# Row sums of a 64 MiB tensor: partition 4a+b holds block a+32b in place of block 4a+b

## The chip, the cores and the metric

The kernel runs on one core of one Trainium2 chip. The metric is the device time of one execution in microseconds, the median of several runs. Before the change it is 160.3 us (three runs, 160.28 to 160.54).

A core has 128 partitions of on-chip memory, five engines with queues of their own (here DVE, ACT, POOL and SP have work; PE has none) and sixteen DMA engines, which move data between HBM and the partitions. SP issues every DMA copy of this kernel.

## The reference

```python
def setup_inputs():
    batch, seq, dim = 32, 512, 1024
    return {
        "x": np.random.randn(batch, seq, dim).astype(np.float32),
        "divisor": float(dim),
    }

def reference(x: np.ndarray, divisor: float) -> np.ndarray:
    return (np.sum(x, axis=-1) / divisor).astype(np.float32)
```

The input is 16,384 rows of 1,024 float32 numbers, 67.1 MB. The output is the sum of each row, divided by 1,024: 16,384 numbers, 64 KiB.

## The kernel before, in words

**How rows are dealt out.** Each of the 128 partitions adds up 128 rows. The rows lie in HBM in two parts. The first part is 128 blocks of F = 15 rows; partition p holds block p (`x_first`, `o_first`). The second part is 128 blocks of W = 113 rows; partition p holds block p here too. Of the 113 rows, the first M = 97 are the main rows (`x_main`, `o_main`) and the last L = 16 the closing rows (`x_last`, `o_last`). Each of these names is an access pattern of the HBM tensor, written out by hand: an offset, and pairs of step and count in elements, the slowest first. `x_main`, for instance, goes in 128 steps of 113 rows and takes contiguous numbers at each.

**Loads.** The list `loads` holds ten copies in the order of issue: two rows per partition, five times 16 rows and once 15 rows of the main part; then the 15 rows of the first part; then the first 10.6 rows and the next 3.7 rows of the closing part. They go in turn into three buffers of 64 KiB per partition (`bulk`). Two more copies bring the rest of the closing part into `pa` (1.3 rows, 5,376 B per partition) and `pb` (0.4 of a row, 1,664 B). Within a partition the bytes of a copy are contiguous in HBM and on chip.

**What sets the order.** It is written out by hand, with a semaphore for each buffer. The first two copies are issued at L116; the function `start_loads_at_once` moves them to the very start of SP's program, ahead of the barrier with which the engines begin. The other eight of the list are issued at L144: the third waits for the first one's data, and each later one waits until DVE (and ACT, where it had a share) is done with the buffer it goes to, and until the earlier data of that buffer have landed. `pa` (L145) and `pb` (L146) are issued right behind. Then SP waits for POOL and issues the store of the 15-row part's results (L148), waits until the copy to `pa` has landed and ACT has added up the head of row 14, issues the store of the main results (`res`, L150), waits for the last two sums, and issues the store of the closing results (`fin`, L238). At the very end it waits for all stores.

**Who adds up.** DVE reduces each list entry's rows with one instruction (L215), but for four rows of the 15-row main load and six of the first part's, which ACT adds up with one activation per row (L183). The closing rows are shared between ACT and DVE; DVE takes them row by row, adding the two halves of a row (`both_halves`, L205), and its last instruction adds up `pb` with what came before of the last row. POOL multiplies `res` and `res0` by 1/1024 (L157, L161); closing rows are scaled as they are added up.

Of the kernel before, what the change touches and what calls it, by code (L numbers as in the profile page):

```python
# [35 lines left out]
def kernel(  # L36
# [6 lines left out]
    nc = tc.nc  # L43
    nc.at_finalize(start_loads_at_once)
    xf = x.flatten_outer_dims()
    N, D = xf.shape
    P = nc.NUM_PARTITIONS
# [4 lines left out]
    F, L = 15, 16  # L52
    M = J - F - L
    W = M + L
    x_first = bass.AP(tensor=x.tensor, offset=0, ap=[[F * D, P], [1, F * D]])
    x_main = bass.AP(tensor=x.tensor, offset=P * F * D, ap=[[W * D, P], [1, M * D]])
    x_last = bass.AP(tensor=x.tensor, offset=P * F * D + M * D, ap=[[W * D, P], [1, L * D]])
    o_first = bass.AP(tensor=out.tensor, offset=0, ap=[[F, P], [1, F]])
    o_main = bass.AP(tensor=out.tensor, offset=P * F, ap=[[W, P], [1, M]])
    o_last = bass.AP(tensor=out.tensor, offset=P * F + M, ap=[[W, P], [1, L]])  # L60

    def room(name, *shape):
        return nc.alloc_sbuf_tensor(name, [P, *shape], F32).ap()
# [10 lines left out]
    c10, c14, c15 = 640, 288, 608  # L74
    ends = [0, 10 * D + c10, 14 * D + c14, 15 * D + c15, 16 * D]
    tail = room("tail", 7 * 256)
    pa, row14 = tail[:, 256 : 256 + ends[3] - ends[2]], tail[:, 255 : 256 + D - c14]
    pb = room("pb", 512)[:, : D - c15 + 2]
# [8 lines left out]
    loads = []  # L87
    sems = {}

    def sem(name):  # L90
        sems[name] = nc.alloc_semaphore(name)
        return sems[name]

    in_bulk = [sem(f"in_bulk{i}") for i in range(3)]
    in_pa, in_pb = (sem(f"in_{n}") for n in ("pa", "pb"))
# [8 lines left out]
    for rows_of, src, dst in ((main, x_main, res), (first, x_first, res0)):  # L104
        j = 0
        for rows, on_act in rows_of:
            t = bulk[len(loads) % 3][:, : rows * D]
            loads.append((t, in_bulk[len(loads) % 3], src[:, j * D : (j + rows) * D], on_act, dst[:, j : j + rows]))
            j += rows
    for k in range(2):  # L110
        t = bulk[len(loads) % 3][:, : ends[k + 1] - ends[k]]
        loads.append((t, in_bulk[len(loads) % 3], x_last[:, ends[k] : ends[k + 1]], 0, None))


    for t, s, src, *_ in loads[:2]:
# [18 lines left out]
    for k, (t, s, src, *_) in enumerate(loads):  # L134
# [7 lines left out]
                nc.sync.wait_ge(act, done_act[k - 3])  # L142
            nc.sync.wait_ge(s, arrived[k] - 16)
        nc.sync.dma_start(out=t, in_=src).then_inc(s, 16)  # L144
    nc.sync.dma_start(out=pa, in_=x_last[:, ends[2] : ends[3]]).then_inc(in_pa, 16)  # L145
    nc.sync.dma_start(out=pb[:, : D - c15], in_=x_last[:, ends[3] : ends[4]]).then_inc(in_pb, 16)  # L146
    nc.sync.wait_ge(pool, 3)
    nc.sync.dma_start(out=o_first, in_=res0).then_inc(out_first, 16)  # L148
    nc.sync.wait_ge(in_pa, 17)
# [4 lines left out]
    k = len(main) - 1  # L154
# [31 lines left out]
    for k, (t, s, src, on_act, dst) in enumerate(loads[:-2]):  # L186
        rows = t.shape[1] // D
# [23 lines left out]
    for k, (t, s, src, on_act, dst) in enumerate(loads[:-2]):  # L211
        m = t.shape[1] // D - on_act
        nc.vector.wait_ge(s, arrived[k])
        rows = t[:, : m * D].rearrange("p (r d) -> p r d", d=D)
# [65 lines left out]
```

## Time and profile before

| what | value |
|---|---|
| median of the runs | 160.3 us |
| span of the profiled execution, first to last instruction | 159.3 us |
| DVE busy | 116.7 us, 73% of the span |
| ACT busy | 18.6 us, 12% |
| POOL busy | 1.0 us |
| read from HBM | 67.11 MB |
| share of the sixteen DMA engines' time with a packet | 98.1% |

The profile is of one execution, whose time outside the profiler is not known; the span is the time from its first to its last instruction, 1.0 us under the median of the runs. The chain of work that ended last is followed back from the last instruction, at each step to what released it; a line of it that says DMA means that an engine waited for that copy to land. In the lists by time, SPq stands for SP's queue, on which copies are issued; the time of such a line is that of the issue, not of the transfer. The windows give the share of time in which the DMA engines had a packet on its way, and the bytes that they moved. A landing is the moment when one of the sixteen DMA engines reports its part of a copy; a copy has landed with the sixteenth.

### The profile page before, as it was taken

Reading aid. Unit: us, or ns where it says so; the run is one execution under the profiler, and the core shown is the slowest. Engines: PE = TensorE matmul, PEld = TensorE weight load, DVE = VectorE, ACT = ScalarE, POOL = GpSimd, SP = SyncE. Lnnn points to the kernel's source line nnn. Section 1 sums busy time; section 2 is a strip of 40 time slices with the busy share of each in tenths; the row PEclk is TensorE's granted clock in tenths of the full one; section 3 lists DMA queues with packets and bytes.
Section 4 is the critical chain, followed back from the end, with each engine's and each line's share of the span. In section 5 each row is a group of like instructions: output and inputs, shape, how many; then the busy total and the mean of one; then the engine's idle time right before and its main releaser. Section 6 shows DMA issues by size and latency. Waiting matters only on the chain.

```text
span 159.3 us, 144 instructions
## 1 busy us (share of the span) xinstructions
DVE 116.7 (73%) x32; ACT 18.6 (12%) x35; POOL 1.0 (1%) x7
## 2 busy tenths in 40 slices
DVE  0500009999499994999949999499989990399296
ACT  3000000000000000000000000000009100392196
POOL 0000000000000000000000000000000001000000
DMA  8996996996996997979969969969996999889894
GB/s 296 494 527 263 527 527 263 527 527 263 527 527 263 527 444 346 527 313 477 527 263 527 527 263 527 494 278 463 494 494 262 478 494 494 350 350 525 344 401 154
DMA packets 2160, 67.18 MB, mean 422 GB/s; under 512 B 624, under 2 KB 752, under 8 KB 880
## 3 DMA queue, kind: packets, MB, share of 16 engines
q1 hardware_dynamic: 2160, 67.18, 98.1%
HBM read 67.11 MB, written 0.07 MB: 422 GB/s over the span
## 4 chain that ended last, share of the span: by engine, by line
DMA 67%; DVE 30%; another core or an unknown queue 1%; issue 0%
DMA bulk<-in_x_dram 67%; DVE res L215 29%; DVE bulk L205 1%; DVE tail L205 0%; DVE pb L205 0%; DVE fin L205 0%
## 5 line engine op out<-in xcount | busy, mean ns | idle before, releaser
L215 DVE TENSOR_REDUCE res<-bulk 128x16 f32<-128x16384 f32 (+3 forms) x8 | 110.0, 13754 | 37.7 <-DMA bulk<-in_x_dram 37.7
L183 ACT ACTIVATE junk<-bulk 128x1024 f32<-128x1024 f32 (+1 forms) x16 | 15.6, 973 | 137.2 <-DMA bulk<-in_x_dram 137.2
L205 DVE CUSTOM_DVE_ANT_0 bulk<-bulk 128x512 f32<-128x512 f32 (+1 forms) x9 | 5.5, 665 | 3.1 <-DMA bulk<-in_x_dram 3.1
L183 ACT ACTIVATION_READ_ACCUMULATOR junk<-bulk 128x1 f32 x16 | 3.0, 187 | 0.0
L183 ACT ACT_TABLE_LOAD x1 | 1.3, 1283 | 1.9 <-PEq L119 1.9
L157 POOL TENSOR_SCALAR res<-res 128x97 f32<-128x97 f32 x1 | 0.5, 465 | 129.8 <-DVE res L215 129.8
L205 DVE DVE_READ_ACCUMULATOR2_ANT fin<- 128x1 f32 x10 | 0.8, 82 | 0.0
L183 ACT ACTIVATE junk<-tail 128x737 f32<-128x737 f32 x1 | 0.8, 789 | 0.0
L205 DVE CUSTOM_DVE_ANT_0 bulk<-bulk,part 128x192 f32<-128x192 f32 x1 | 0.4, 420 | 0.3 <-DMA bulk<-in_x_dram 0.3
L205 DVE CUSTOM_DVE_ANT_0 tail<-tail 128x304 f32<-128x304 f32 x1 | 0.5, 476 | 0.0
L205 DVE CUSTOM_DVE_ANT_0 pb<-pb 128x209 f32<-128x209 f32 x1 | 0.4, 379 | 0.1
L161 POOL TENSOR_SCALAR res<-res 128x15 f32<-128x15 f32 x1 | 0.3, 262 | 15.6 <-DVE res L215 15.6
L183 ACT ACTIVATION_READ_ACCUMULATOR junk<-tail 128x1 f32 x1 | 0.2, 187 | 0.0
L153 POOL MEMSET pb<- 128x2 f32 x1 | 0.1, 99 | 1.5 <-POOLq L119 1.5
L261 POOL MEMSET const-bfloat16-1.0<- 128x1 bf16 x1 | 0.1, 101 | 0.0
L261 POOL MEMSET const-uint8-127<- 128x1 uint8 x1 | 0.1, 101 | 0.0
L261 POOL MEMSET const-float32-0.0<- 128x1 f32 x1 | 0.1, 98 | 0.2 <-issue 0.2
L261 POOL MEMSET const-float32-1.0<- 128x1 f32 x1 | 0.1, 98 | 0.0
L205 DVE DVE_READ_ACCUMULATOR2_ANT pb<- 128x1 f32 x1 | 0.1, 84 | 0.0
L205 DVE DVE_READ_ACCUMULATOR2_ANT part<- 128x1 f32 x1 | 0.1, 83 | 0.0
## 6 DMA issues: line engine op xcount, KB each, us to landing
bulk<-in_x_dram SPq DMA_DIRECT2D x2, 7680.0 KB, 39.3
bulk<-in_x_dram SPq DMA_DIRECT2D x1, 5440.0 KB, 32.0
bulk<-in_x_dram SPq DMA_DIRECT2D x1, 1872.0 KB, 23.5
bulk<-in_x_dram SPq DMA_DIRECT2D x1, 1024.0 KB, 4.6
tail<-in_x_dram SPq DMA_DIRECT2D x1, 672.0 KB, 24.7
pb<-in_x_dram SPq DMA_DIRECT2D x1, 208.0 KB, 24.8
bulk<-in_x_dram SPq DMA_DIRECT2D x5, 40.8
out_dram<-res SPq DMA_DIRECT2D x1, 48.5 KB, 1.6
```

The lines of the kernel that those rows point to most:

```text
L153: nc.gpsimd.memset(pb[:, D - c15 :], 0.0).then_inc(pool)
L157: nc.gpsimd.tensor_scalar_mul(out=res, in0=res, scalar1=scale).then_inc(pool)
L161: nc.gpsimd.tensor_scalar_mul(out=res0, in0=res0, scalar1=scale).then_inc(pool)
L183: nc.scalar.activation(scratch, src, COPY, scale=by, accum_out=dst).then_inc(count)
L205: return nc.vector.tensor_tensor_reduce(out=src[:, :h], in0=src[:, :h], in1=src[:, h:], scale=by, scalar=ahead, op0=ADD, op1=ADD, accum_ou ...
L215: nc.vector.reduce_sum(out=dst[:, :m], in_=rows, axis=AX).then_inc(dve)
L261: nc = _bacc.Bacc("TRN2", target_bir_lowering=False, num_devices=1)
```

## The change

In the 113-row part the partitions hold other blocks. Where partition p held block p, partition 4a + b (a from 0 to 31, b from 0 to 3) now holds block a + 32b. So partitions 0, 1, 2, 3 hold blocks 0, 32, 64, 96, and partitions 4 to 7 hold blocks 1, 33, 65, 97. The access patterns in HBM say this with one pair more: 32 steps of one block, and in each four steps of 32 blocks. The stores of `res` and `fin` use the same mapping, so that each sum goes to its row. On the chip's side nothing is addressed otherwise, and the 15-row part is as before. Slices of the patterns take the last axis whatever the number of axes.

```diff
     x_first = bass.AP(tensor=x.tensor, offset=0, ap=[[F * D, P], [1, F * D]])
-    x_main = bass.AP(tensor=x.tensor, offset=P * F * D, ap=[[W * D, P], [1, M * D]])
-    x_last = bass.AP(tensor=x.tensor, offset=P * F * D + M * D, ap=[[W * D, P], [1, L * D]])
+    G = P // 4
+    x_main = bass.AP(tensor=x.tensor, offset=P * F * D, ap=[[W * D, G], [G * W * D, 4], [1, M * D]])
+    x_last = bass.AP(tensor=x.tensor, offset=P * F * D + M * D, ap=[[W * D, G], [G * W * D, 4], [1, L * D]])
     o_first = bass.AP(tensor=out.tensor, offset=0, ap=[[F, P], [1, F]])
-    o_main = bass.AP(tensor=out.tensor, offset=P * F, ap=[[W, P], [1, M]])
-    o_last = bass.AP(tensor=out.tensor, offset=P * F + M, ap=[[W, P], [1, L]])
+    o_main = bass.AP(tensor=out.tensor, offset=P * F, ap=[[W, G], [G * W, 4], [1, M]])
+    o_last = bass.AP(tensor=out.tensor, offset=P * F + M, ap=[[W, G], [G * W, 4], [1, L]])
...
-            loads.append((t, in_bulk[len(loads) % 3], src[:, j * D : (j + rows) * D], on_act, dst[:, j : j + rows]))
+            loads.append((t, in_bulk[len(loads) % 3], src[..., j * D : (j + rows) * D], on_act, dst[:, j : j + rows]))
...
-        loads.append((t, in_bulk[len(loads) % 3], x_last[:, ends[k] : ends[k + 1]], 0, None))
+        loads.append((t, in_bulk[len(loads) % 3], x_last[..., ends[k] : ends[k + 1]], 0, None))
...
-    nc.sync.dma_start(out=pa, in_=x_last[:, ends[2] : ends[3]]).then_inc(in_pa, 16)
-    nc.sync.dma_start(out=pb[:, : D - c15], in_=x_last[:, ends[3] : ends[4]]).then_inc(in_pb, 16)
+    nc.sync.dma_start(out=pa, in_=x_last[..., ends[2] : ends[3]]).then_inc(in_pa, 16)
+    nc.sync.dma_start(out=pb[:, : D - c15], in_=x_last[..., ends[3] : ends[4]]).then_inc(in_pb, 16)
```

## The prediction

> **What bounds the kernel now.** I read the profile's page first, for who is busy. The vector engine is busy for 73% of the span, the DMA engines for all of it.
>
> ```profile
> span 159.3 us, 144 instructions
> DVE 116.7 (73%) x32; ACT 18.6 (12%) x35; POOL 1.0 (1%) x7
> DMA packets 2160, 67.18 MB, mean 422 GB/s; under 512 B 624, under 2 KB 752, under 8 KB 880
> q1 hardware_dynamic: 2160, 67.18, 98.1%
> ```
>
> 98.1% is the share of sixteen engines' time in which a packet was on its way. Next I read the windows by stage, which say where the rest is lost (columns: stretch, its length, busy time of DVE, ACT and POOL, granted clock, DMA share, GB/s).
>
> ```profile
> 1.00:4.60 3.60, 0.00 (x0) 1.28 (x1) 0.10 (x1) 1.00 1.48 580
> 4.60:43.28 38.68, 19.51 (x2) 0.00 (x0) 0.00 (x0) 1.00 1.00 434
> 43.28:81.98 38.70, 34.44 (x3) 0.00 (x0) 0.00 (x0) 1.00 1.00 434
> 81.98:119.83 37.85, 34.44 (x2) 0.00 (x0) 0.00 (x0) 1.00 0.99 428
> 119.83:138.00 18.17, 11.90 (x2) 4.28 (x9) 0.47 (x1) 1.00 0.96 417
> ```
>
> A packet's bytes are booked where it starts, so the first window is too high (580) and those at the end too low; the long windows are right. From 4.6 to 82 us the sixteen engines move 434 GB/s, share 1.00. The trace's list of packets gives the same: a packet of 65,536 B (one partition's share of a sixteen-row load; 640 of them) takes 2.418 us at the least and at the median, 27.1 GB/s an engine and 434 GB/s for sixteen. So 67.11 MB need 154.7 us, and nothing but the bytes, the start and the end decide the time. The chain of work and the instructions in order of time (both: start, length, what) give these two ends.
>
> ```profile
> 0.00 4.58 DMA bulk<-in_x_dram
> ...
> 131.75 23.51 DMA bulk<-in_x_dram
> ...
> 157.41 0.02 issue
> 157.44 0.38 DVE pb L205
> ```
>
> ```profile
> 0.00 0.85 SPq L116 DMA_DIRECT2D bulk<-in_x_dram  x2
> ...
> 157.85 0.33 SPq L238 DMA_DIRECT2D out_dram<-fin  x1
> ```
>
> At the start SP issues the first load in 0.376 us (the shorter of the two at L116; the second takes 0.424), and the list of packets has the first one at 1.00 us: 0.62 us later. At the end the last input bytes land at 157.41, DVE adds them up by 157.82, SP issues the store of `fin` from 157.85 to 158.18, its packets run from 158.68 to 158.88, and it lands at 159.26. The span of this execution is 159.3; the median of the runs is 160.3, so 1.0 us lies outside the span, and I carry that over.
>
> Between these ends, 157.41 - 1.00 - 154.7 = 1.7 us are lost. The list of packets accounts for half: summed over packets, each against the shortest of its size, an engine spends 0.48 us too much in the first load's 8,192 B packets (309 ns undisturbed, 602 on average for the first sixteen), 0.18 in those of 61,440 B, 0.15 in those of 65,536 B. The rest is gaps and engines that do not end together (the last load's sixteen landings are spread over 0.56 us).
>
> **The change, part by part.** No instruction of DVE, ACT, POOL or PE is added, removed or moved, and SP issues the same fifteen copies in the same order with the same bytes. Three things differ.
>
> *Which bytes a partition gets.* Nothing in the sums depends on it: every row is added up within a partition, and results are written by the same mapping. Cost 0 on the compute engines: 8 reductions (110.0 us), 16 activations (15.6) as before, all under the loads but for the last 0.4 us, which depend on no address.
>
> *Where in HBM the engines read at one time.* A step from one partition to the next was one block of 113 rows, 452 KiB; now it is 32 blocks, 14.1 MiB, and a step of four partitions, which was 1,808 KiB, is 452 KiB. Every run is as long as before (16 rows, 64 KiB). Bounds: a gain of at most the 1.7 us lost now; a loss of as much as the stretch seen now, 0.8 us, doubled (nearest rows: the 8,192 B packets, which are hardest hit). The row nearest to most of these bytes is the 65,536 B packet, which with the old addresses is at its floor in the median and 3.6 ns above it in the mean: there is next to nothing to win in the bulk. I take -0.05 us (a tenth of the first load's stretch).
> The Trainium skill bears on this in "DMA: Bandwidth & Descriptors", section "Latency and other measured facts": copies whose partitions lie a large power of two apart lose up to half their rate, and a pad of 4 KiB brings it back. Neither 452 nor 1,808 KiB is such a pitch, so by that rule the sum has 0 here in place of -0.05; the trace of before agrees for 1,808 KiB with its 434 GB/s.
>
> *The form of the copies.* In the new program the DRAM side of thirteen of the fifteen copies (the eleven input loads of the 113-row part and the stores of `res` and `fin`) has three steps, 32 x 4 x length, where it had two, 128 x length; the load and the store of the 15-row part keep theirs. The program built from before also marks each copy as one whose pattern is worked out ahead; the thirteen lose that mark. SP's sequencer then has more to work out per issue. No row shows an issue of that kind. Bounds from the rows: at the least 0; at the most one whole further issue, that is 0.376 us for the first load and 0.332 for the last store. A gain is excluded, since no part of an issue goes away. A copy that is issued right behind another is the nearest row for an issue that finds its work not ready: 0.43 and 0.44 us at L145 and L146 against 0.328 for one that stood alone, so 0.1 us is a lower mark; a whole address pattern more on each side is nearer to a second issue than to that, so I take 0.25 us each, and keep 0 and the full issue for the range.
>
> Now copy by copy. The first load (L116): nothing is ahead of it, so its 0.25 us shift the first packet from 1.00 to 1.25 and with it every byte, since the engines never rest: **+0.25**. The second load at L116, queued behind it, is issued by about 1.35 in place of 0.85; the first load keeps the engines to 4.3, so 3 us cover it. SP's barrier stands behind both: the other engines would start at 2.4 rather than 1.9, and DVE has nothing to do before 4.6. The eight at L144: each is issued 18 us or more ahead of its first byte (at 4.6 and 6.9 for bytes from 23.6 and 42.9; at 131.7 for 150.3); this lead covers 0.25 us many times over. What waits behind them on SP are the next copies, which wait for DVE anyway: 95.6 us in seven waits. L145 and L146 are issued at 132.1 and 132.6 and land at 157: covered by some 23 us. The store of the 15-row part is unchanged. The store of `res` (L150) is issued at 156.89 for 0.34 us, and SP waits from 157.23 to 157.85 for `fin`: 0.62 us of cover, so 0.25 more are free, and at twice the cost still; were that gone, the store of `fin` would slip. Its landing, at 158.45, would be 158.70, before that of `fin`. The store of `fin` (L238) is the last thing on the path and has no cover: **+0.25**. Its 64 B runs and the 388 B runs of `res` go to the same outputs from other partitions; their packets take 11 and 24 ns, and I put 0 on that.
>
> Sum: 159.3 + 0.25 + 0.25 - 0.05 = 159.75 span, plus 1.0 outside it: **160.8 us**, 0.3% above 160.3.
>
> **The rivals.** *The addresses win more than the issue costs (faster).* The stretch of the first load falls away where neighbouring DMA engines read 452 KiB apart in place of 1,808, and engines finish closer together. For it: the 0.48 us of the first packets and the 0.56 us spread at the end are there to be won. Against: the first packets of any engine are also the ones that start from an idle memory, which no address cures, and the long packets are at their floor. At half of the 1.7 us, 0.85, and 0.5 for the issues: 160.3 - 0.35 = 159.95. It decides when the saving passes 0.5 us; without any issue cost it would be 159.45.
>
> *The form is free and the addresses do not matter (no change).* For it: SP's issue may be overlapped with the 0.62 us to the first packet; before's packets show no sign of addresses. Then 160.3. Against: SP's 0.33 to 0.44 us are visible and serial at both ends.
>
> *The copies are dealt out unevenly.* Sixteen landings per copy say that sixteen engines share 128 partitions. If 32 x 4 were dealt out so that two engines serve what one port takes, or eight engines did all the work, the thirteen copies' 113/128 of 154.7 us would double: 136.6 more, 297 us. It decides already when one engine gets a ninth partition: an eighth of 136.6 is 17 us, 177 us. For it: no row shows such a copy. Against: 32 and 128 are both whole multiples of sixteen.
> The Trainium skill's "DMA: Bandwidth & Descriptors", section "Why a DMA increments its semaphore by 16 and not by 1", states that the number of engines is the largest up to 16 that divides the slowest steps of both sides; by it 32 and 128 give 16, and the time stays 160.8. Its section "The descriptor swizzle" gives engine 0 partitions 0 to 3 and 32 to 35, which 32 steps of four can be cut into; no run here shows it yet.
>
> **How the numbers follow.** Forecast 0.60; faster by addresses 0.22; no change 0.10; uneven 0.08 (with anything else that slows the stream by a per cent or more). A measurement of this kernel tells 0.2% (0.3 us) from no change. The forecast's own range is 160.3 to 161.1 (0 to 0.71 for the two issues, with the stretch a little either way); of it about a tenth falls within 0.2%. The low end goes to the faster rival's 159.95, rounded to 159.9, which leaves out the half of it that saves more. The high end: both issues doubled, 161.0, and the stretch of 0.8 us grown by three quarters, 161.6. What is left out: about 0.11 below and 0.08 above. Faster 0.22; same 0.16 (0.10 and a tenth of the forecast); slower 0.62 (0.54 and 0.08).
>
> **What would show it.** SP's issue of the first load should take about 0.6 us in place of 0.376, that of `fin` likewise, and the other loads' issues too, but not the one of the 15-row load. The first landing at 4.58 should come at about 4.8, the last reduction start about 0.2 us later, and the windows from 5 to 82 us should still say 434 GB/s. If the issues stand at 0.33 us, the step on the form is wrong; if the long windows move off 434, the step on the addresses is wrong; if the first landing comes before 4.58 with longer issues, the first packets have won by the addresses.

## The result, and the profile after

The changed kernel takes 161.45 us (median of five runs, 161.31 to 161.57) against 160.33 us for the kernel before on the same chip: a ratio of 1.0067, 95% interval 1.0055 to 1.0079. It is slower by about 1.1 us, on the side that was forecast, inside the stated range (159.9 to 161.6), but above the forecast of 160.8 and above the forecast's own range (160.3 to 161.1).

The page of the changed kernel shows the same work and the same busy times:

```profile
span 160.0 us, 144 instructions
DVE 116.7 (73%) x32; ACT 18.7 (12%) x35; POOL 1.0 (1%) x7
q1 hardware_dynamic: 2160, 67.18, 97.6%
```

The packets and bytes are those of before; only their share of the span fell, from 98.1% to 97.6%. The windows by stage (stretch, its length, busy time of DVE, ACT and POOL, granted clock, DMA share, GB/s) say that the long middle is as fast as it was:

```profile
4.60:43.28 38.68, 19.51 (x2) 0.00 (x0) 0.00 (x0) 1.00 1.00 432
43.28:81.98 38.70, 34.44 (x2) 0.00 (x0) 0.00 (x0) 1.00 1.00 434
81.98:119.83 37.85, 34.44 (x2) 0.00 (x0) 0.00 (x0) 1.00 1.01 436
```

In the trace's list of packets a 65,536 B packet still takes 2.418 us at the median, and each copy still reports sixteen landings. So the time came from the two ends. First the chain of work, then SP's queue by time (start, length, what):

```profile
0.00 5.21 DMA bulk<-in_x_dram
...
131.97 23.54 DMA bulk<-in_x_dram
...
157.70 0.02 issue
157.72 0.38 DVE pb L206
```

```profile
0.00 1.30 SPq L117 DMA_DIRECT2D bulk<-in_x_dram  x2
...
132.56 0.60 SPq L146 DMA_DIRECT2D tail<-in_x_dram  x1
133.20 0.60 SPq L147 DMA_DIRECT2D pb<-in_x_dram  x1
148.49 0.35 SPq L149 DMA_DIRECT2D out_dram<-res  x1
157.14 0.61 SPq L151 DMA_DIRECT2D out_dram<-res  x1
158.14 0.57 SPq L239 DMA_DIRECT2D out_dram<-fin  x1
```

The two first issues take 1.30 us together, where they took 0.85, and the first load lands at 5.21 in place of 4.58. L149, the store of the 15-row part, keeps its old form and its old 0.35 us; L146, L147, L151 and L239, all in the new form, take 0.57 to 0.61. For the eight loads that are issued later, the answer by line gives least, median and greatest duration in ns, first the kernel before and then the changed one:

```profile
L144 SPq DMA_DIRECT2D bulk<-in_x_dram x8: 328/328/328, 4.6 to 131.7; - x8
```

```profile
L145 SPq DMA_DIRECT2D bulk<-in_x_dram x8: 372/535/541, 5.2 to 132.0; - x8
```

The one at 372 ns is the 15-row load, which kept two steps and its mark; the other seven went from 328 to about 535.

### The profile page after: what moved, and what is told of

Its sections match the earlier page's. It is cut to its first block, busy times and chain, and to the rows that moved or that the text cites. A ratio compares the mean times of both kernels' runs of the same rounds, so it can differ in the third digit from the quotient of the medians.

```text
span 160.0 us, 144 instructions
## 1 busy us (share of the span) xinstructions
DVE 116.7 (73%) x32; ACT 18.7 (12%) x35; POOL 1.0 (1%) x7
## 3 DMA queue, kind: packets, MB, share of 16 engines
q1 hardware_dynamic: 2160, 67.18, 97.6%
## 4 chain that ended last, share of the span: by engine, by line
DMA 67%; DVE 30%; another core or an unknown queue 1%; issue 0%
DMA bulk<-in_x_dram 67%; DVE res L216 29%; DVE bulk L206 1%; DVE pb L206 0%; DVE tail L206 0%; DVE fin L206 0%
```

## The experiments

All are small edits of the kernel before or of the changed one. In each the ratio is to runs of the kernel before on the same chip. It is not the quotient of the two medians given beside it; microseconds given as "about" are worked out from the ratio, and the difference of the medians is up to 0.14 us away from them. The theory held going in is "issue": all the time is lost at the two ends, because an unmarked copy in three steps reaches its first packet later. The main rivals are "bulk addresses" (the new blocks cost or win time in the long loads) and, within "issue", whether the mark, the third step or the new blocks are what costs.

### The first load alone

```diff
+    G = P // 4
+    x_new = bass.AP(tensor=x.tensor, offset=P * F * D, ap=[[W * D, G], [G * W * D, 4], [1, W * D]])
...
-            loads.append((t, in_bulk[len(loads) % 3], src[:, j * D : (j + rows) * D], on_act, dst[:, j : j + rows]))
+            loads.append((t, in_bulk[len(loads) % 3], x_new[..., : rows * D] if not loads else src[:, j * D : (j + rows) * D], on_act, dst[:, j : j + rows]))
```

> The kernel before, with the first load alone (two rows) in the new three-step form and from the new blocks; the sums of these two rows therefore stand in other rows' places. Theory 'issue' (the time is lost at the two ends, in SP's issue of an unmarked three-step copy): issue of the first load about 0.67 us, first landing at about 5.2 us, all later landings of the bulk 0.3 to 0.6 late, 160.8 to 160.9 us. Theory 'bulk addresses' (the time is lost in the long loads): 160.3 us, first landing at 4.6. Theory 'free start' (only the end costs): 160.3.

Measured: 161.06 us against 160.42, ratio 1.0031 (1.0021 to 1.0041), about 0.50 us. The chain and SP's queue:

```profile
0.00 5.58 DMA bulk<-in_x_dram
...
157.90 0.02 issue
```

```profile
0.00 1.26 SPq L118 DMA_DIRECT2D bulk<-in_x_dram  x2
...
158.34 0.33 SPq L240 DMA_DIRECT2D out_dram<-fin  x1
```

The first issue takes 0.633 us and the first packet is at 1.41 us. The long loads are the old ones, and still everything down to the last load ends late. The first landing was expected at about 5.2 us and came at 5.58: that is 4.17 us after the first packet, where the kernel before has 3.58 and 3.82 in its two profiles (the second one follows below). The issue theory accounts for the first packet's 0.41 us and not for the rest of this landing's delay. One copy of 1 MB out of 67 does this: "bulk addresses" and "free start" fall as explanations of this half.

### The last store alone

```diff
-    o_last = bass.AP(tensor=out.tensor, offset=P * F + M, ap=[[W, P], [1, L]])
+    G = P // 4
+    o_last = bass.AP(tensor=out.tensor, offset=P * F + M, ap=[[W, G], [G * W, 4], [1, L]])
```

> The kernel before, with the last store (fin) alone in the new form; its sums therefore stand in other rows' places. Theory 'issue': the issue takes 0.57 in place of 0.33 us, the landing comes 1.8 in place of 1.4 us after its start, 160.5 to 160.7 us. Theory 'bulk addresses': 160.3.

Measured: 160.92 us against 160.42, ratio 1.0027 (1.0016 to 1.0038), about 0.43 us; the number expected was too low, the mechanism is as expected. SP's queue:

```profile
0.00 0.85 SPq L117 DMA_DIRECT2D bulk<-in_x_dram  x2
...
157.68 0.63 SPq L239 DMA_DIRECT2D out_dram<-fin  x1
```

The issue is 0.30 us longer (0.632 for 0.332), and the landing comes 1.86 us after its start instead of 1.41, so 0.45 later. Nothing lies behind this store, so all of it is paid.

### The ten loads between, without the ends

`x_new` is that of the first experiment.

```diff
-            loads.append((t, in_bulk[len(loads) % 3], src[:, j * D : (j + rows) * D], on_act, dst[:, j : j + rows]))
+            loads.append((t, in_bulk[len(loads) % 3], x_new[..., j * D : (j + rows) * D] if loads and src is x_main else src[:, j * D : (j + rows) * D], on_act, dst[:, j : j + rows]))
...
-        loads.append((t, in_bulk[len(loads) % 3], x_last[:, ends[k] : ends[k + 1]], 0, None))
+        loads.append((t, in_bulk[len(loads) % 3], x_new[..., M * D + ends[k] : M * D + ends[k + 1]], 0, None))
...
-    nc.sync.dma_start(out=pa, in_=x_last[:, ends[2] : ends[3]]).then_inc(in_pa, 16)
-    nc.sync.dma_start(out=pb[:, : D - c15], in_=x_last[:, ends[3] : ends[4]]).then_inc(in_pb, 16)
+    nc.sync.dma_start(out=pa, in_=x_new[..., M * D + ends[2] : M * D + ends[3]]).then_inc(in_pa, 16)
+    nc.sync.dma_start(out=pb[:, : D - c15], in_=x_new[..., M * D + ends[3] : M * D + ends[4]]).then_inc(in_pb, 16)
```

> The kernel before, with the new form and the new blocks in ten input loads of the 113-row part, and not in the first load nor in the stores; the sums of these ten loads' rows therefore stand in other rows' places. Theory 'issue': 160.3 us, for SP's issues of the ten loads (0.53 to 0.60 us in place of 0.33 to 0.44) are covered. Theory 'bulk addresses', as a loss: 161 or more. As a gain (the 0.3 us that the changed kernel won back between 44 and 120 us come from the addresses): 159.9 to 160.1, with the landing at about 119.8 earlier by 0.3.

Measured: 160.50 us against 160.42, ratio 1.0005 (0.9996 to 1.0015): no difference. This holds both the longer issues of ten loads and the new blocks for 98% of the 113-row part's bytes. The issues did get longer, and they are covered:

```profile
4.84 127.19 SPq L146 DMA_DIRECT2D bulk<-in_x_dram  x8
132.09 0.60 SPq L147 DMA_DIRECT2D tail<-in_x_dram  x1
132.74 0.60 SPq L148 DMA_DIRECT2D pb<-in_x_dram  x1
```

```profile
4.60:43.28 38.68, 19.50 (x2) 0.00 (x0) 0.00 (x0) 1.00 1.00 434
43.28:81.98 38.70, 34.44 (x2) 0.00 (x0) 0.00 (x0) 1.00 1.00 434
```

So longer issues and new addresses together are worth at most 0.04% on the faster side and 0.15% on the slower, and no run here points to a version faster than the kernel before. The three parts, 0.31, 0.27 and 0.05%, each with an interval of about 0.1% either way, add up to 0.63%, against 0.67% for the whole change. The store of `res`, also in the new form there, is in none of the three; in the changed kernel its issue ends at 157.75 us, before that of `fin` begins at 158.14, and it lands at 159.13, before `fin` at 159.94.

### Old form and old blocks, without the mark

```diff
     nc = tc.nc
+    nc.dge_precook = False
```

> The kernel before in everything, two steps and old blocks, but with the mark of a pattern worked out ahead taken from all fifteen copies. Theory 'issue, by the mark': SP's issues take 0.55 to 0.67 us, first landing at about 5.2, landing of fin 1.7 to 1.8 us after its issue, 161.0 to 161.5 us. Theory 'issue, by the three steps': issues stay at 0.33 to 0.44 and the time at 160.3. Theory 'addresses' (first packets slower because of the new blocks): longer issues shift the first packet by 0.3, first landing 4.9, 160.6 to 160.9.

Measured: 161.16 us against 160.42, ratio 1.0039 (1.0027 to 1.0051), about 0.63 us, without a single address or step changed. SP's queue:

```profile
0.00 1.21 SPq L117 DMA_DIRECT2D bulk<-in_x_dram  x2
...
148.38 0.51 SPq L149 DMA_DIRECT2D out_dram<-res  x1
157.06 0.50 SPq L151 DMA_DIRECT2D out_dram<-res  x1
158.05 0.47 SPq L239 DMA_DIRECT2D out_dram<-fin  x1
```

"By the mark" holds for most of the cost: issues that stood at 328 ns take 472, and the first packet of the first load comes at 1.35 us. The lengths were expected at 0.55 to 0.67 and are 0.47 to 0.60, since the third step is missing here; it adds its own part (535 ns in the changed kernel where this one has 472). The first load lands at 5.19, as the mark's theory expected, and not at 4.9. No run here has three steps with the mark.

### The kernel before, profiled again

> The kernel before, unchanged, profiled once more, to see how far its first profile stands for it. If the 0.18 us of stretched 61,440 B packets and the late sixteenth landing (0.31 us behind the fifteenth at 101.5 and 119.8 us) were of that one execution: a span of about 159.0 us, run time 1.35 us above the span as in e1 to e4, no such gap between the last two landings. If they belong to the old blocks: the span stays at 159.3 and the gap shows again. Time 160.3 to 160.4 either way.

Measured: 160.49 us against 160.53, ratio 0.999 (0.998 to 1.000), which also shows how far two samples of one kernel can differ. Its span is 159.1 us, 1.34 us below that run's time of 160.42; in the changed kernel and in the first four experiments the same difference is 1.33 to 1.35 us.

```profile
0.00 4.83 DMA bulk<-in_x_dram
...
131.52 23.51 DMA bulk<-in_x_dram
...
157.20 0.02 issue
157.22 0.38 DVE pb L205
```

The sixteenth landing at 119.6 us is 0.04 us behind the fifteenth, not 0.31, and the stretch of the 61,440 B packets is 0.03 us an engine, not 0.18. The first, second and fourth experiment, which read the long loads from the old blocks, do not show it either (0.03 to 0.11 us and 0.03 to 0.04 us). So these two marks were of the first profile's one execution. What looked like 0.4 us won back by the changed kernel between 44 and 120 us (0.60 us late at 43.86, 0.22 at 120.03) was the reference losing it: against the repeated profile the changed kernel is 0.38 us late at 43.86 and 0.45 at 120.03.

### The changed kernel with its start undone

The 15-row part becomes a 17-row part, and the first load takes its two rows from there, in the old form. All results are at their places.

```diff
-    F, L = 15, 16
+    F, L = 17, 16
...
-    main = [(2, 0)] + [(16, 0)] * 5 + [(15, 4)]
-    first = [(15, 6)]
+    main = [(16, 0)] * 5 + [(15, 4)]
+    first = [(2, 0), (15, 6)]
...
-    for rows_of, src, dst in ((main, x_main, res), (first, x_first, res0)):
-        j = 0
+    for rows_of, src, dst, j in (
+        (first[:1], x_first, res0, 0), (main, x_main, res, 0), (first[1:], x_first, res0, first[0][0])
+    ):
...
-    k = len(main) - 1
+    k = len(main)
...
-    k += len(first)
+    k += 1
```

> The changed kernel with one part undone: the 15-row part becomes a 17-row part (the other 111 rows), and the first load takes its two rows from it, in two steps and with the mark; all other loads of the 111-row part and the stores of res and fin keep the new form. Theory 'issue': the cost of the start goes and that of the last store stays: first issue 0.38 us, first landing 4.6 to 4.8, fin landing 1.8 us after its issue, 160.7 to 160.9 us. Theory 'it is the new blocks or their pitch': 161.3 to 161.5 as the changed kernel.

Measured: 160.95 us against 160.53, ratio 1.0020 (1.0010 to 1.0030), where the changed kernel stands at 1.0067. The time is a little above the 160.7 to 160.9 expected, on a chip where the kernel before stands at 160.53. The first issue is back at 0.382 us and the first packet at 1.03; the store is as slow as in the changed kernel:

```profile
0.00 5.00 DMA bulk<-in_x_dram
```

```profile
0.00 1.07 SPq L118 DMA_DIRECT2D bulk<-in_x_dram  x2
...
157.77 0.57 SPq L240 DMA_DIRECT2D out_dram<-fin  x1
```

The first landing, at 5.00, is later than the 4.6 to 4.8 expected; the issue theory does not say why, and I leave it open (the 8,192 B packets were stretched by 0.65 us an engine here; in the four executions with an old first load, 0.48 to 0.63). The landing of the last input, at 157.34, is within 0.14 us of the repeated profile's 157.20 all the same.

### Three steps, nearly the old blocks

```diff
+    G = P // 4
+    x_near = bass.AP(tensor=x.tensor, offset=P * F * D, ap=[[4 * W * D, G], [(W + 1) * D, 4], [1, 2 * D]])
...
-            loads.append((t, in_bulk[len(loads) % 3], src[:, j * D : (j + rows) * D], on_act, dst[:, j : j + rows]))
+            loads.append((t, in_bulk[len(loads) % 3], x_near if not loads else src[:, j * D : (j + rows) * D], on_act, dst[:, j : j + rows]))
```

> The kernel before, with the first load alone in three steps, but from nearly the old addresses: partition 4a+b reads rows b and b+1 of block 4a+b (so three of four partitions take the wrong two rows, at most 12 KiB off). Theory 'form': as e1, first packet at 1.41 us, 160.8 to 161.1. Theory 'new blocks' for the part of e1 that goes beyond the unmarked two-step copy of e4: first packet at 1.35, first landing at 5.2 rather than 5.6, 160.6 to 160.8.

Measured: 160.93 us against 160.53, ratio 1.0024 (1.0013 to 1.0036). The issue takes 0.633 us and the first packet is at 1.41, the same to the ns and to 5 ns as with the new blocks; the first landing is at 5.45. SP's queue and the chain:

```profile
0.00 1.26 SPq L118 DMA_DIRECT2D bulk<-in_x_dram  x2
```

```profile
0.00 5.45 DMA bulk<-in_x_dram
```

The form is what costs at the start, not where the blocks lie. The time by itself does not decide between the two expectations, whose ranges meet at 160.8; the first packet and the landing do.

## Why the prediction was right, and where it was too small

The path from an issue to its first packet, from the trace's lists of issues and packets (us):

| kernel | first load: issue | to first packet | store of `fin`: issue | to first packet | ratio of times |
|---|---|---|---|---|---|
| before, two profiles | 0.376, 0.376 | 1.00, 1.01 | 0.332, 0.332 | 0.83, 0.83 | 1 |
| no mark, two steps | 0.572 | 1.35 | 0.472 | 1.13 | 1.0039 |
| changed: no mark, three steps | 0.667 | 1.44 | 0.573 | 1.22 | 1.0067 |

**The form of the copies** was the step that decides, and the cover was right for each copy: ten loads in the new form cost nothing in the third experiment, the first load and the last store cost theirs in the first two (0.50 and 0.43 us). The rows chosen for bounds held the issue itself: 0.29 and 0.24 us more against the 0.25 taken, within 0 and 0.376 or 0.332. They did not hold what the path pays, the delay of the first packet. What failed is the size of the term, because it was taken to be the issue's length alone. The step "its 0.25 us shift the first packet from 1.00 to 1.25" should have read 1.44: behind the end of an unmarked issue the first packet comes another 0.15 us later (0.77 us for 0.62 at the start, 0.65 for 0.50 at the store). So the two terms measure 0.43 and 0.39 in place of 0.25 and 0.25, both above the upper bounds of 0.376 and 0.332.

**The range.** That 161.45 still lies inside the stated range is luck. Its upper end went from 161.0, both issues doubled, to 161.6 by a stretch of the packets that was to grow by three quarters. The stretch of the first packets did not grow (0.51 us an engine in the changed kernel, 0.48 and 0.60 in the two profiles of before), and what filled the room kept for it was other time: 0.15 us behind each issue, and the rest that the next paragraph leaves open.

**The sum.** The forecast added 0.45 us. The runs say 1.1, with an interval of 0.9 to 1.3. The two ends as measured make 0.83; against the repeated profile of before, the last input lands 0.50 us later (157.70 for 157.20) and the store lands 0.40 us later after its issue, 0.90 together, which is the difference of the spans, 160.0 and 159.1 (against the first profile's 159.3 it is 0.7). The 0.07 beyond the first packet's delay goes with engines that end the same copy farther apart (0.68 us between the first and the last landing of `pb`, 0.40 in the repeated profile). What remains up to 1.1 is inside the intervals and is not attributed. Nor is all of the step from the unmarked kernel to the changed one: 0.28% or 0.45 us, of which the first packets show 0.18.

**The base.** "1.0 us lies outside the span" was wrong in size: it is about 1.34 in every run with both numbers. By that the profiled execution of before took some 160.6 us, above its median; this is inferred, since its own time is not given, but other executions of this kernel with a span of 159.3 took 160.63 to 160.67. It did not move the forecast's difference, but part of the 1.7 us "lost between the ends" was that one execution's: in the repeated profile the same difference is 157.20 - 1.01 - 154.7 = 1.5.

**Addresses.** "I take -0.05" is not seen: ratio 1.0005 with ten loads moved, from 0.06 us faster to 0.24 slower, an interval too wide to exclude so small a gain. The stretch of the first packets, 0.48 us in the first profile of before, is 0.51 in the changed kernel and 0.60 in the repeated profile of before: it differs as much between executions as between kernels, and is no reserve that addresses can win. With that the rival on the faster side falls. The Trainium skill's rule in "DMA: Bandwidth & Descriptors", section "Latency and other measured facts", is that row pitches at large powers of two cost bandwidth. The traces agree as far as they go: steps of 1,808 and of 452 KiB between groups of four partitions both run at 434 GB/s; no run here has such a power of two.

**Uneven dealing** fell: sixteen landings per copy and the old packet sizes at the old speed. By the Trainium skill's "DMA: Bandwidth & Descriptors", section "Why a DMA increments its semaphore by 16 and not by 1", 32 and 128 steps give sixteen engines, and the trace agrees with its sixteen landings. **The form is free** fell with the first, second and fourth experiment.

Of the signs named ahead, the first issue at "about 0.6" came out at 0.667 and `fin` at 0.573; the 15-row load, which was to keep its 0.328, took 0.372, still far from the 0.535 of the others, and why is open; the long windows kept 434 within 2. The first landing, named at 4.8, came at 5.21. The last reduction, named at about 0.2 later, began at 157.72: 0.28 later than in the first profile of before and 0.50 later than in the repeated one.

## What to carry to other kernels

In this kernel, where a stream of copies keeps the DMA engines busy, the first copy's issue and the last store's issue stand bare, and all others are covered. In a kernel of the same build, look there first for what a change of an access pattern costs, and try to keep these two in the plainest form even when the rest needs a richer one. Such a kernel, with every sum at its place, was not run here: the third experiment has its time (ratio 1.0005) and not its results, the sixth undoes the start alone. Read the time to the first packet, not the issue's length alone. Before an effect of a few tenths of a microsecond is read out of two profiles, take the reference's profile twice.

## What had not been expected

An address pattern's form costs beyond its issue: without the mark the first packet comes 0.15 us later after the issue has ended, at the load and at the store alike, and with two steps as with three. A third step by itself adds 0.06 us to an issue in the middle of the stream (535 for 472 ns) and 0.1 us at both ends of the changed kernel. Where a single copy has the new form, at the start or at the end, its issue takes 0.633 and 0.632 us against 0.667 and 0.573, so the length also depends on the program around it. And the time between the landings of one copy can last: in the changed kernel the sixteenth landing is 0.17 us behind the fifteenth at the first load and 0.27 behind at `pb`, 152 us later. It need not last: with the start undone, the sixteen landings are spread over 0.70 us at the first load and 0.53 at `pb`.
